# A hybrid decoder layer on one core: memory-branch gates in seven-product groups, and four of eight k-pairs by seven products in the projections and gates

## The chip, the cores and the metric

The program runs on one core of a Trainium2 chip. The core has a matrix engine (PE, TensorE), whose weight loads are listed apart as PEld, a vector engine (DVE), a scalar engine (ACT), a general engine (POOL) and a queue engine (SP) that issues the DMAs. Products accumulate in PSUM, which holds eight banks of 128 x 512 numbers; everything else on the core lies in SBUF. The metric is device time in microseconds (us), lower is better. A matmul here has a stationary operand of 128 x 128 and a moving one of 128 x 512.

## The reference

One decoder layer on 256 tokens with 2048 features. All arithmetic is float32.

```python
x = x + swiglu_half_ffn(x, ffn1_norm, ffn1_w_gate_up, ffn1_w_down)
h = rmsnorm(x, mix_norm)
u_pool, q_f, k_f, v_f, f_logit, q_m, gate_logit = jnp.split(h @ w_in, split_idx, axis=-1)
y_pool = pool_mixer(u_pool, pool_w, pool_scale) @ w_pool_up
y_fox  = forgetting_attention(rmsnorm(q_f), rmsnorm(k_f), v_f, log_f) @ w_fox_o
k_m, v_m = jnp.split(rmsnorm(mem, mem_norm) @ w_mem_kv, 2, axis=-1)
y_mem  = memory_attention(rmsnorm(q_m), rmsnorm(k_m), v_m) @ w_mem_o
g_pool, g_fox, g_mem = jnp.split(jax.nn.sigmoid(gate_logit), 3, axis=-1)
x = x + (g_pool * y_pool + g_fox * y_fox + g_mem * y_mem) @ w_out
x = x + swiglu_half_ffn(x, ffn2_norm, ffn2_w_gate_up, ffn2_w_down)
```

`w_in` is 2048 x 10768; its last 6144 columns are the three gates, 2048 columns each. The FFNs have 5632 hidden features.

## The kernel before

**Products.** The 256 tokens are two tiles of 128 (t = 0, 1). The 2048 features that a product sums over are 16 k-tiles of 128, that is eight k-pairs. A left operand is held as its high and low part (`fp32r`), and every weight tile is cut in the same way: ACT writes the high part `wh` from the loaded `raw`, DVE subtracts and writes the low part `wl` (`cut`, L238 and L239; in `mm_group` L343 and L344). One float32 product is then three matmuls, high by high, high by low and low by high. `mm_group` makes 512 columns from all k-tiles: 96 matmuls for 16 k-tiles and both token tiles, recorded at L350.

**Groups with seven products.** `pair_group` makes 2 x 512 columns at once. A k-pair, the two token tiles and the two column blocks are a 2 x 2 by 2 x 2 block product, and with sums of blocks it takes seven block products in place of eight: 21 matmuls in place of 24, all recorded at L244. The sums on the left side (`forms`) are made once for each k-pair by `form_page` (L219 to L227). The sums on the weight side are made each time: for a seven-product k-pair DVE writes `ta` (1024 columns), two halves of `tb` (512 each), and the low parts `wl` (1024), `hal` (1024), `wl` (512) and `hbl` (1024), and ACT writes the high parts `wh`, `hah`, `wh` (512) and `hbh`. A plain k-pair of the group costs DVE two `wl` of 1024. After the last seven-product k-pair ACT and four DVE operations (L314 to L318) form four terms, which L597 (projection), L905 (gates) or L387 (output) add to the four plain sums. The group holds all eight PSUM banks: four plain sums and four of the seven products.

**Which k-pairs.** The third argument from the end, an order of k-pairs, and the forms that exist set it. `MIXED = (3, 0, 4, 1, 5, 2, 6, 7)` with forms 0, 1 and 2 puts the seven-product pairs at positions 1, 3 and 5, each between plain ones. It is used for ten groups in each FFN, for the projection `kf`, for the gates of the last branch (fox) and for the second half of `w_out`.

**The order of the layer between the FFNs.** Projections `qf` (`mm_group`), `kf` (`pair_group`), `km`, the columns of the forget logits and `qm`, `vm`, `u_pool`, `vf`; then for each of three branches, in the order pool, memory, fox, and for each half of 1024 columns, the gates, their sigmoid on ACT, and `merge`: the product of the branch's output with its weight, times the gate, added to `acc`. Small work (transposes, attention, forms) waits in a queue `side`; `tick()` takes one step of it, `drain()` all. `mm_group` ticks after every two k-tiles. `pair_group` ticks twice after each plain k-pair that stands behind the last seven-product one. Behind `kf` stands a `drain()`: what is left of the transposes of the memory tokens (`memT`) and of `qf` (`qT`) is made there, and the next product, `km`, needs `memT`.

**Buffers and order.** Pages of 4 KB per partition come from a pool of 30 (x1, forms, acc, `ta`, `tb`, `hah`, `hal`, `hbh`, `hbl` and more), `raw` has 3 buffers, `wh` and `wl` 5 each, temporaries 8. Instructions are put in order on each engine by the recording layer, which runs its own model of time over them; on the chip each engine takes its list in that order.

Of the kernel before, what the change touches and what calls it, by code (L numbers as in the profile page):

```python
# [21 lines left out]
FF = 5632  # L22
NFC = FF // 512
DOWN = (2, 5, 8, 11, 14)
MIXED = (3, 0, 4, 1, 5, 2, 6, 7)
KF = FF // P
EPS = 1e-6
# [6 lines left out]
def hybrid_layer(  # L34
# [37 lines left out]
    side = deque()  # L72
# [20 lines left out]
    def temp(shape, name, dtype=F32):  # L93
        return tp.tile([P, *shape], dtype, tag="t", name=name)
# [312 lines left out]
    def form_steps(forms, tiles, n=3):  # L407
        return [lambda j=j: form_page(forms, tiles, j) for j in range(n)]
# [140 lines left out]
    cb, x1, rs, s1 = residual(s0, G_MIX, "x1")  # L549
    lx = lhs_of(x1)  # L550
# [35 lines left out]
    def project(w, c0, ncol, lhs, r, name, forms=None):  # L586
# [3 lines left out]
        else:  # L590
            buf = pages(T, [ncol], F32, name)
        if forms:
            acc, terms = pair_group(w, c0, c0 + 512, lhs, forms, MIXED)
            for g in range(2):
                for t in range(T):
                    d = terms[t, g]
                    nc.vector.tensor_tensor(d, acc[t, g], d, ALU.add)  # L597
                    nc.scalar.activation(
                        buf[t][:, g * 512 : (g + 1) * 512], d, AF.Copy, scale=r[0][:, t : t + 1]
                    )  # L600
            return buf
# [9 lines left out]
    win = w_in[0]  # L611
# [10 lines left out]
                )  # L622

    forms1 = {}
    side.extend(form_steps(forms1, x1))
    side.append(load_mem)
    side.extend(pause)
    for c in range(4):
# [238 lines left out]
    acc = pages(4, [T, 512], F32, "acc")  # L867
    mg = []
# [3 lines left out]
        (w_fox_o[0], 8, lhs_of(yf), D),  # L872
    )
    for i, (w, kt, ly, off) in enumerate(branches):
        if i == 2:
            drain()
        for c0 in range(0, 4, 2):
            gates = {}

            def sigmoid(c, src):  # L880
                gates[c] = []
                for t in range(T):
                    g = src[t] if i == 2 else temp([512], "gate")
                    nc.scalar.activation(g, src[t], AF.Sigmoid, scale=rs[0][:, t : t + 1])
                    gates[c].append(g)

# [9 lines left out]
                if i == 2:  # L896
                    side.extend(to_lhs(mg, lambda t, c=c: acc[c][:, t, :], None, "mg"))

            if i == 2:
                o = 4112 + off + c0 * 512  # L900
                pg, terms = pair_group(win, o, o + 512, lx, forms1, MIXED)
                for n in range(2):
                    for t in range(T):
                        d = terms[t, n]
# [11 lines left out]
    cb, x2, rs, s2 = residual(s1, G_FFN2, "x2")  # L916
    lg = lhs_of(mg)
    formsg, forms2 = {}, {}
    side.extend(form_steps(formsg, mg))
    for c in range(2):  # L920
        s1.load(c)
        ps = mm_group(w_out[0], c * 512, KD, lg)
        cb(c, [[ps[t][0]] for t in range(T)])
    for c in range(2, 4):
        s1.load(c)
    po, terms = pair_group(w_out[0], 1024, 1536, lg, formsg, MIXED)
    side.extend(pause * 2)
    for n in range(2):
        cb(2 + n, sums(po, terms, n))
# [41 lines left out]
```

## Time and profile before

| | |
|---|---|
| device time, three runs | 2133.16, 2136.04, 2136.01 us, median 2136.01 |
| the profiled execution | 2136.36 us, span 2134.5 us, mean granted clock 0.998 |
| PE, PEld, DVE, ACT busy | 2122.8, 1752.7, 1690.6, 1171.3 us |
| instructions on PE, DVE, ACT | 9710, 2151, 1466 |
| HBM read | 426.16 MB, 208 GB/s over the span |

The profiled execution is 1.9 us longer than its span and 0.35 us longer than the median. In a row of the timeline the first number is the start, the second the duration; in brackets stands how long the engine sat idle before it and what ended that. In the chain of work that ended last, a row is a start, a length and the line that the chain ran through. Matmuls overlap, so the time of one is read as a stretch divided by its count, not from a single row.

### The profile page before, as it was taken

What the parts mean: (1) busy time and instruction counts of PE and PEld (TensorE: products, weight loads), DVE (VectorE), ACT (ScalarE), POOL (GpSimd) and SP (SyncE); (2) the same over time, 40 slices, a digit from 0 to 9 for tenths busy, and PEclk for the clock granted to TensorE, in tenths of its full rate; (3) what the DMA queues carried; (4) which work ended last, traced back from release to release, by engine and by line L of the source; (5) the groups of instructions that cost most, each with busy time, mean ns of one, the idle gap of its engine ahead of it and who ended that gap; (6) DMA issues with size and microseconds to landing.
All of it is one profiled execution on the core that took longest, in us unless ns stands there. A gap on an engine that the chain in (4) does not pass through costs nothing.

```text
span 2134.5 us, 26003 instructions
## 1 busy us (share of the span) xinstructions
PE 2122.8 (99%) x9710; PEld 1752.7 (82%) x9710; DVE 1690.6 (79%) x2151; ACT 1171.3 (55%) x1466; POOL 3.5 (0%) x24
## 2 busy tenths in 40 slices
PE   9999999999999999999999999999999999999999
PEld 6888888888888888887788888888888888888887
DVE  6888898889858788657645778688899889989675
ACT  6555555556545565555644555555555555556453
POOL 0000000000000000000000000000000000000000
PEclk9999999999999999999999999999999999999999
DMA  7666666666866664754455656765666666677764
GB/s 257 207 207 207 207 217 208 211 230 228 272 211 205 225 203 141 255 163 158 139 195 189 195 178 212 234 224 200 210 213 205 221 208 213 206 235 246 259 190 151
DMA packets 221090, 444.66 MB, mean 208 GB/s; under 512 B 12238, under 2 KB 13348, under 8 KB 220964
## 3 DMA queue, kind: packets, MB, share of 16 engines
q1 hardware_dynamic: 220672, 442.96, 63.0%
q8 instruction: 76, 1.25, 0.2%
q14 instruction: 50, 0.41, 0.1%
q10 hardware_dynamic: 292, 0.05, 0.0%
HBM read 426.16 MB, written 16.79 MB: 208 GB/s over the span
## 4 chain that ended last, share of the span: by engine, by line
PE 99%; DVE 1%; DMA 1%; ACT 0%; issue 0%; SPq 0%; DVEq 0%; ACTq 0%
PE mm L244 68%; PE mm L350 27%; PE hid L426 1%; DMA raw<-in_ffn_w_gate_up_dram 0%; PE x L200 0%; PE fpt L849 0%; DVE wl L344 0%; PE fav L859 0%; PE mg L200 0%; PE flg L821 0%; PE mav L754 0%; PE mlg L727 0%; PE flg L819 0%; PE fav L861 0%; DVE xr L387 0%; PE fav L860 0%
## 5 line engine op out<-in xcount | busy, mean ns | idle before, releaser
L238 ACT ACTIVATE wh<-raw 128x1024 fp32r<-128x1024 f32 (+1 forms) x560 | 552.6, 989 | 580.1 <-PE mm L244 344.2
L239 DVE TENSOR_TENSOR wl<-raw,wh 128x1024 fp32r<-128x1024 f32 (+1 forms) x560 | 629.5, 1134 | 187.9 <-ACT wh L238 186.8
L244 PE MATMUL mm<-wh,x 128*128 128x512 f32 x2116 | 656.1, 391 | 0.0
L244 PEld LDWEIGHTS mm<-wh,x 128*128 128x128 f32 x2116 | 394.1, 188 | 80.0
L244 PE MATMUL mm<-wl,x 128*128 128x512 f32 x1058 | 410.9, 390 | 0.0
L344 DVE TENSOR_TENSOR wl<-raw,wh 128x1024 fp32r<-128x1024 f32 (+2 forms) x217 | 255.7, 1181 | 161.5 <-ACT wh L343 160.8
L350 PE MATMUL mm<-wh,x 128*128 128x512 f32 (+1 forms) x1216 | 371.9, 384 | 3.0 <-ACT wh L343 1.7
L244 PE MATMUL mm<-wh,hid 128*128 128x512 f32 x1168 | 357.8, 390 | 0.0
L343 ACT ACTIVATE wh<-raw 128x1024 fp32r<-128x1024 f32 (+2 forms) x217 | 221.1, 1024 | 237.4 <-PE mm L350 183.2
L350 PEld LDWEIGHTS mm<-wh,x 128*128 128x128 f32 x1216 | 224.7, 188 | 48.4 <-issue 2.9
L244 PEld LDWEIGHTS mm<-wh,hid 128*128 128x128 f32 x1168 | 218.8, 188 | 45.2
L244 PEld LDWEIGHTS mm<-wl,x 128*128 128x128 f32 x1058 | 198.6, 188 | 41.9
L350 PE MATMUL mm<-wl,x 128*128 128x512 f32 (+1 forms) x608 | 231.5, 382 | 0.5 <-DVE wl L344 0.5
L244 PE MATMUL mm<-wl,hid 128*128 128x512 f32 x584 | 222.4, 389 | 0.0
L350 PEld LDWEIGHTS mm<-wl,x 128*128 128x128 f32 x608 | 114.5, 188 | 21.6 <-DVE wl L344 1.0
L290 DVE TENSOR_TENSOR ta<-raw 128x1024 f32<-128x1024 f32 x92 | 112.3, 1220 | 20.5 <-DMA raw<-in_ffn_w_gate_up_dram 8.0
L244 PEld LDWEIGHTS mm<-wl,hid 128*128 128x128 f32 x584 | 109.6, 188 | 22.7
L238 ACT ACTIVATE hah<-ta 128x1024 fp32r<-128x1024 f32 x92 | 96.9, 1053 | 37.5 <-DVE ta L290 37.5
L239 DVE TENSOR_TENSOR hal<-ta,hah 128x1024 fp32r<-128x1024 f32 x92 | 112.4, 1222 | 3.4 <-ACT hah L238 3.4
L239 DVE TENSOR_TENSOR hbl<-tb,hbh 128x1024 fp32r<-128x1024 f32 x92 | 112.3, 1221 | 0.1
L244 PE MATMUL mm<-hah,form 128*128 128x512 f32 x368 | 111.3, 389 | 0.0
L238 ACT ACTIVATE hbh<-tb 128x1024 fp32r<-128x1024 f32 x92 | 96.8, 1052 | 21.9 <-DVE tb L296 21.9
(324 smaller groups left out, 2143.3 us busy)
## 6 DMA issues: line engine op xcount, KB each, us to landing
raw<-in_ffn_w_gate_up_dram SPq DMA_DIRECT2D x321, 512.0 KB, 4.0
raw<-in_ffn_w_down_dram SPq DMA_DIRECT2D x176, 512.0 KB, 5.5
raw<-in_w_in_dram SPq DMA_DIRECT2D x52, 1024.0 KB, 5.0
raw<-in_w_in_dram SPq DMA_DIRECT2D x48, 512.0 KB, 4.2
raw<-in_ffn_w_gate_up_dram SPq DMA_DIRECT2D x15, 1024.0 KB, 7.3
hd<-hf SPq DMA_DIRECT2D x20, 512.0 KB, 5.2
hg<-hd SPq DMA_DIRECT2D x20, 512.0 KB, 8.4
raw<-in_w_mem_kv_dram SPq DMA_DIRECT2D x8, 1024.0 KB, 7.6
```

The lines of the kernel that those rows point to most:

```text
L238: nc.scalar.activation(dst[0], src, AF.Copy)
L239: nc.vector.tensor_tensor(dst[1], src, dst[0].bitcast(F32), ALU.subtract)
L244: nc.tensor.matmul(ps, sides[part], wt[i][:, col : col + 512], start=start and q == 0, stop=stop and q == 2)
L290: nc.vector.tensor_tensor(ta, s[:, 3:4, :].to_broadcast([P, 2, 512]), s[:, 1:3, :], ALU.add)
L343: nc.scalar.activation(hv, rv, AF.Copy)
L344: nc.vector.tensor_tensor(lv, rv, hv.bitcast(F32), ALU.subtract)
L350: nc.tensor.matmul(ps[t][i][:, :n], lhs(k, part, t), wt[:, kk, o : o + n], start=k == 0 and q == 0, stop=k == kt - 1 and q == 2,)
L426: nc.tensor.transpose(ps[:, j, t * P : (t + 1) * P], hd[t][:, k * P : (k + 1) * P], ident)
```

## The change

The memory branch (i = 1) takes its gates through `pair_group`, as the fox branch does, with the sigmoid written over the terms. A new order `HALF = (4, 0, 5, 1, 6, 2, 3, 7)` with a fourth form puts seven-product pairs at positions 1, 3, 5 and 6; the `kf` projection, the gates of the memory and fox branches and the second half of `w_out` use it. The FFNs keep `MIXED` and three forms. The drain that stood before the third branch stands before the second and the third.

```diff
+HALF = (4, 0, 5, 1, 6, 2, 3, 7)
...
         if forms:
-            acc, terms = pair_group(w, c0, c0 + 512, lhs, forms, MIXED)
+            acc, terms = pair_group(w, c0, c0 + 512, lhs, forms, HALF)
...
-    side.extend(form_steps(forms1, x1))
+    side.extend(form_steps(forms1, x1, 4))
...
-        if i == 2:
+        if i > 0:
             drain()
...
-                    g = src[t] if i == 2 else temp([512], "gate")
+                    g = src[t] if i > 0 else temp([512], "gate")
...
-            if i == 2:
+            if i > 0:
                 o = 4112 + off + c0 * 512
-                pg, terms = pair_group(win, o, o + 512, lx, forms1, MIXED)
+                pg, terms = pair_group(win, o, o + 512, lx, forms1, HALF)
...
-    side.extend(form_steps(formsg, mg))
+    side.extend(form_steps(formsg, mg, 4))
...
-    po, terms = pair_group(w_out[0], 1024, 1536, lg, formsg, MIXED)
+    po, terms = pair_group(w_out[0], 1024, 1536, lg, formsg, HALF)
```

One line is added at the top, so a line of the changed kernel is one higher than the same line before. In the built programs PE has 9604 matmuls and transposes before and 9568 after, DVE 2153 and 2241 instructions, ACT 1408 and 1436, SP 753 and 769. The 16 more on SP are loads of the memory gates, cut in 512 KB pieces instead of 1 MB.

Three places show how the order moves. First DVE at the end of `kf`: `raw_6624` holds the third seven-product pair, `ta_6631`, `tb_6632`, `hal_6635` and `hbl_6645` are made from it, `wl_6887` to `wl_6943` are the weights of `km`, and the row of L315 is the first term. Before:

```order
L570 TENSOR_TENSOR qf_5984<-qf_5984,qfy_6402 128x1024
L239 TENSOR_TENSOR hal_6635<-ta_6631,hah_6634 128x1024
L295 TENSOR_TENSOR tb_6632<-ta_6631,raw_6624 128x512
L239 TENSOR_TENSOR wl_6757<-raw_6727,wh_6756 128x1024
L344 TENSOR_TENSOR wl_6887<-raw_6884,wh_6886 128x1024
L296 TENSOR_TENSOR tb_6632<-tb_6632,raw_6624 128x512
L344 TENSOR_TENSOR wl_6903<-raw_6884,wh_6902 128x1024
L239 TENSOR_TENSOR hbl_6645<-tb_6632,hbh_6644 128x1024
L190 SCALAR_TENSOR_TENSOR memT_6717<-memT_6718,cols_108,memT_6717 128x256 x2
L344 TENSOR_TENSOR wl_6921<-raw_6918,wh_6920 128x1024
L315 TENSOR_TENSOR u3_6670<-mm_6502,ua_6669 128x512
```

After, from the same `hbl_6645` on; `raw_6669` holds the fourth seven-product pair, `raw_6904` and `raw_6938` hold weights of `km`:

```order
L240 TENSOR_TENSOR hbl_6645<-tb_6632,hbh_6644 128x1024
L291 TENSOR_TENSOR ta_6676<-raw_6669 128x1024
L345 TENSOR_TENSOR wl_6907<-raw_6904,wh_6906 128x1024
L345 TENSOR_TENSOR wl_6923<-raw_6904,wh_6922 128x1024
L240 TENSOR_TENSOR hal_6680<-ta_6676,hah_6679 128x1024
L296 TENSOR_TENSOR tb_6677<-ta_6676,raw_6669 128x512
L345 TENSOR_TENSOR wl_6941<-raw_6938,wh_6940 128x1024
L345 TENSOR_TENSOR wl_6963<-raw_6938,wh_6962 128x1024
L297 TENSOR_TENSOR tb_6677<-tb_6677,raw_6669 128x512
L240 TENSOR_TENSOR hbl_6690<-tb_6677,hbh_6689 128x1024
L191 SCALAR_TENSOR_TENSOR memT_6742<-memT_6743,cols_108,memT_6742 128x256 x2
L316 TENSOR_TENSOR u3_6715<-mm_6502,ua_6714 128x512
```

A whole further set of sums now stands between `hbl` of the third pair and the first term, with four weight cuts of `km` in between.

Second PE at the same place: the last matmuls of `kf` (`hbl,form` closes a product that the terms need), then the transposes `memT` and `qT`, then `km`. Before:

```order
L244 MATMUL mm<-hbl,form 128x512
L244 MATMUL mm<-hbl,x_5319 128x512
L244 MATMUL mm<-wh,x_6093 128x512 x2
L244 MATMUL mm<-wl,x_6093 128x512
L244 MATMUL mm<-wh,x_6093 128x512 x2
L244 MATMUL mm<-wl,x_6093 128x512
L244 MATMUL mm<-wh,x_6119 128x512 x2
L244 MATMUL mm<-wl,x_6119 128x512
L244 MATMUL mm<-wh,x_6119 128x512 x2
L244 MATMUL mm<-wl,x_6119 128x512
L200 MATMUL memT<-ident,mraw 128x128 x12
L580 MATMUL qT<-ident,qf 128x128 x16
```

After:

```order
L245 MATMUL mm<-hah,form 128x512 x4
L245 MATMUL mm<-hal,form 128x512 x2
L245 MATMUL mm<-hbh,form 128x512 x2
L245 MATMUL mm<-hbh,x_5345 128x512 x2
L245 MATMUL mm<-hbl,form 128x512
L245 MATMUL mm<-hbl,x_5345 128x512
L245 MATMUL mm<-wh,x_6119 128x512 x2
L245 MATMUL mm<-wl,x_6119 128x512
L245 MATMUL mm<-wh,x_6119 128x512 x2
L245 MATMUL mm<-wl,x_6119 128x512
L201 MATMUL memT<-ident,mraw 128x128 x16
L581 MATMUL qT<-ident,qf 128x128 x16
```

The fourth pair's sums are used 12 matmuls before the end of the group, six matmuls stand behind the last of them instead of twelve, and 16 transposes of `memT` instead of 12 stand before `qT`.

Third DVE in the memory gates. Before, where one merge ends and the next gates begin:

```order
L344 TENSOR_TENSOR wl_9920<-raw_9917,wh_9919 128x1024
L344 TENSOR_TENSOR wl_9936<-raw_9917,wh_9935 128x1024
L894 TENSOR_TENSOR gate_9837<-mm_9841,gate_9837 128x512
L894 TENSOR_TENSOR gate_9839<-mm_9842,gate_9839 128x512
L895 TENSOR_TENSOR acc_8189<-acc_8189,gate_9837 128x512
L895 TENSOR_TENSOR acc_8189<-acc_8189,gate_9839 128x512
L344 TENSOR_TENSOR wl_9954<-raw_9951,wh_9953 128x1024
L344 TENSOR_TENSOR wl_9970<-raw_9951,wh_9969 128x1024
L344 TENSOR_TENSOR wl_9988<-raw_9985,wh_9987 128x1024
L344 TENSOR_TENSOR wl_10004<-raw_9985,wh_10003 128x1024
```

After, in the middle of the first memory group, where the third and fourth seven-product pairs (`raw_9558`, `raw_9603`) follow each other:

```order
L291 TENSOR_TENSOR ta_9565<-raw_9558 128x1024
L240 TENSOR_TENSOR wl_9543<-raw_9523,wh_9542 128x1024
L240 TENSOR_TENSOR wl_9562<-raw_9558,wh_9561 128x1024
L240 TENSOR_TENSOR wl_9573<-raw_9558,wh_9572 128x512
L240 TENSOR_TENSOR hal_9569<-ta_9565,hah_9568 128x1024
L296 TENSOR_TENSOR tb_9566<-ta_9565,raw_9558 128x512
L240 TENSOR_TENSOR wl_9607<-raw_9603,wh_9606 128x1024
L297 TENSOR_TENSOR tb_9566<-tb_9566,raw_9558 128x512
L240 TENSOR_TENSOR wl_9618<-raw_9603,wh_9617 128x512
L240 TENSOR_TENSOR hbl_9579<-tb_9566,hbh_9578 128x1024
```

DVE's list there turns from weight cuts alone into cuts mixed with sums, and the cuts of the fourth pair stand among the sums of the third.

## Rows read from the trace of the kernel before

**Rows 1.** The page's part 1: busy us, share of the span, instructions.

```profile
PE 2122.8 (99%) x9710; PEld 1752.7 (82%) x9710; DVE 1690.6 (79%) x2151; ACT 1171.3 (55%) x1466; POOL 3.5 (0%) x24
```

**Rows 2.** The page's part 4: the chain that ended last, by engine.

```profile
PE 99%; DVE 1%; DMA 1%; ACT 0%; issue 0%; SPq 0%; DVEq 0%; ACTq 0%
```

**Rows 3.** Chain of the gates and merges: start, length, line, matmuls.

```profile
1062.01 147.37 PE mm L350 x649
1209.38 41.48 PE mm L244 x183
```

**Rows 4.** Stretches: us, then busy us by engine, granted clock, DMA share, GB/s.

```profile
1100.00:1209.00 109.00, 109.00 (x483) 90.28 (x482) 61.78 (x61) 48.96 (x50) 0.00 (x0) 1.00 0.60 193
1508.81:1551.26 42.45, 42.45 (x193) 35.15 (x192) 37.40 (x42) 24.11 (x28) 0.00 (x0) 1.00 0.66 211
766.87:808.72 41.85, 41.85 (x188) 34.54 (x188) 39.05 (x54) 24.89 (x31) 0.00 (x0) 1.00 0.60 200
816.00:818.00 2.00, 2.00 (x6) 1.55 (x5) 2.00 (x5) 2.00 (x5) 0.00 (x0) 0.50 0.00 0
```

**Rows 5.** Chain around the end of kf.

```profile
766.87 32.93 PE mm L244 x145
...
813.38 0.70 DVE u L597
...
814.13 0.66 PE qT L580 x4
814.79 3.60 PE mm L350 x8
```

**Rows 6.** Timeline of PE at the end of kf.

```profile
808.72 1.47 PE L200 MATMUL memT<-ident,mraw 128*128 128x128 f32 x12
810.68 1.26 PE L580 MATMUL qT<-ident,qf 128*128 128x128 f32 x8 [0.50 <-DVE u L317]
813.40 1.38 PE L580 MATMUL qT<-ident,qf 128*128 128x128 f32 x8 [1.47 <-DVE uv L318]
814.73 0.68 PE L350 MATMUL mm<-wh,memT 128*128 128x512 f32 x1
```

**Rows 7.** Timeline of DVE in kf, from the first seven-product pair's ta.

```profile
767.31 1.22 DVE L290 TENSOR_TENSOR ta<-raw 128x1024 f32<-128x1024 f32 x1
...
795.84 1.22 DVE L239 TENSOR_TENSOR hal<-ta,hah 128x1024 fp32r<-128x1024 f32 x1
796.98 0.69 DVE L295 TENSOR_TENSOR tb<-ta,raw 128x512 f32<-128x512 f32 x1
797.58 1.22 DVE L239 TENSOR_TENSOR wl<-raw,wh 128x1024 fp32r<-128x1024 f32 x1
...
801.83 1.22 DVE L239 TENSOR_TENSOR hbl<-tb,hbh 128x1024 fp32r<-128x1024 f32 x1
...
806.89 0.68 DVE L315 TENSOR_TENSOR u<-mm,ua 128x512 f32<-128x512 f32 x1
...
813.99 0.68 DVE L597 TENSOR_TENSOR uv<-mm,uv 128x512 f32<-128x512 f32 x1
```

**Rows 8.** Timeline of ACT in kf.

```profile
797.38 1.06 ACT L343 ACTIVATE wh<-raw 128x1024 fp32r<-128x1024 f32 x1 [3.10 <-DMA raw<-in_w_mem_kv_dram]
...
800.57 1.06 ACT L238 ACTIVATE hbh<-tb 128x1024 fp32r<-128x1024 f32 x1
```

**Rows 9.** Timeline of SP: loads of the memory weights.

```profile
792.24 10.06 SPq L331 DMA_DIRECT2D raw<-in_w_mem_kv_dram  x4
```

**Rows 10.** The page's part 6: issues, KB each, median us to landing.

```profile
raw<-in_w_mem_kv_dram SPq DMA_DIRECT2D x8, 1024.0 KB, 7.6
```

**Rows 11.** Timeline of DVE at the end of w_out.

```profile
1413.96 0.69 DVE L315 TENSOR_TENSOR u<-mm,ua 128x512 f32<-128x512 f32 x1 [0.51 <-PE mm L244]
...
1430.06 0.68 DVE L387 TENSOR_TENSOR xr<-uv,xr 128x512 f32<-128x512 f32 x1
```

**Rows 12.** Timeline of PE at the end of w_out.

```profile
1437.67 1.47 PE L200 MATMUL x<-ident,xr 128*128 128x128 f32 x12
```

## The prediction, written before the changed kernel was run

> **What bounds the kernel now.** The page's busy times come first: PE works 99% of the span, its weight loads 82%, DVE 79%, and the span has 9710 PE instructions [rows 1]. The chain that ended last says the same: 99% of it runs through PE [rows 2]. So a matmul taken away is worth its own time, wherever PE is not then made to wait for somebody else. The price is a stretch of the chain divided by its count: 147.37 us over 649 matmuls of `mm_group` is 0.2271 us, 41.48 us over 183 of `pair_group` is 0.2267 us [rows 3]. The question is whether PE stays fed, and by whom. The stretches show who is next behind PE [rows 4]. In a pass of plain gates (1100 to 1209) DVE is busy 61.78 of 109 us, 57%. In a group of FFN2 with three seven-product pairs it is busy 37.40 of 42.45 us, 88%, and in `kf` 39.05 of 41.85 us, 93%; in all three PE is busy every microsecond. So seven-product pairs spend DVE's reserve, and at 93% it still just holds.
>
> The one place that the change touches where PE does wait today is the end of `kf`. The chain leaves PE there for DVE's last adds [rows 5]. PE's timeline shows how: the last matmul of `kf` ends at about 808.7, twelve `memT` transposes follow, then eight `qT` transposes wait 0.50 us for `u` of L317 and eight more wait 1.47 us for `uv` of L318 [rows 6]. All eight PSUM banks are held by four sums and four products; a bank comes free only when DVE has read it into a term or an add. `km` starts at 814.73, right behind DVE's last add, which runs from 813.99 for 0.68 us [rows 7].
>
> **The change part by part.** *Matmuls.* PE loses 36: three in `kf`, 24 in the memory gates (two passes of 192 become 180), six in the fox gates, three in `w_out`. By 0.2267 us they are worth 8.16 us. I take the three of `kf` out, since DVE sets that group's end (below): 33 x 0.2267 = 7.5 us of gain.
>
> The Trainium skill (TensorE: Matmul & The Clock Gate, section Back-to-back issue gap) gives about 131 ns as the sustained spacing of matmuls of 512 columns in a real kernel. By that figure 33 matmuls would be worth an estimated 4.3 us. The trace does not agree: 649 of them in one gapless row took 227 ns each [rows 3], and the measurement decides.
>
> *Memory and fox gates.* One DVE operation of 1024 columns costs 1.14 us (795.84 to 796.98), one of 512 columns 0.60 us (796.98 to 797.58) [rows 7]. A seven-product pair takes four of the first and three of the second, 6.4 us; a plain pair takes two, 2.3 us. On PE a seven-product pair is 21 x 0.2267 = 4.8 us, a plain one 5.4 us. A memory pass (180 matmuls of gates, 48 of the merge) is then 228 x 0.2267 = 51.7 us of PE. DVE's list over it has 28 operations of each size: 28 x 1.14 + 28 x 0.60 = 48.7 us, 94%. This is what `kf` carries now with PE gapless [rows 4]. The doubtful point is the third and fourth pair side by side (third place of the order): walking both lists with these prices, every DVE product still stands some 3 to 6 us ahead of the matmul that uses it, the least at `hbl` of the fourth pair. I take 0; what hides it is the 57% of the pass before, in which PE is fed so easily that the buffers are full when the gates begin. Without that cover it costs what rival two says. A fox pass has 62.6 us of PE and, by the same count, at most 54.3 us of DVE, 87%, so 0 there. The 16 more loads on SP are the same bytes in halves: 0.
>
> *The drains.* The one that now stands before the memory branch finds an empty list, since the fox attention's steps are all taken in the pool branch: 0. The extra form step costs DVE and ACT a few short operations in stretches of 57% load: 0.
>
> *The end of `kf`.* Here DVE has no reserve. From the first `ta` at 767.31 to the end of the third pair's `hbl`, which starts at 801.83 [rows 7], 35.7 us passed. The list holds 23 operations of 1024 and 8 of 512 columns there, 31.0 us, which leaves 4.7 us for 16 short operations and the waits. In the changed order the list up to the *fourth* pair's `hbl` holds 27 and 11: 37.4 us. With the same 4.7 us it ends at 767 + 42.1 = 809. Two more waits are likely. ACT's `hbh` takes 1.06 us [rows 8] and stands between `tb` and `hbl`, with nothing else left in DVE's list: 1.1 us. And `wl_6907`, a weight cut of `km`, stands ahead of the fourth pair's sums (first place of the order). Its load can start only when the last plain pair has left its buffer, at about 795.5. Today's first `km` load was issued at 792.24 [rows 9], and ACT, which waited 3.10 us for it, began its `wh` at 797.38 [rows 8]: 5.1 us. So the load lands at 800.6, `wh` is done at 801.7, and DVE stands there at 800.9 or so: 1.0 us. `hbl` then ends at 811.0, while PE, which without any wait would end `kf` at 808.4, stands idle behind it for five to six microseconds.
>
> From there: today 7.84 us pass from the first term at 806.89 [rows 7] to `km`, that is eight operations of 0.60, two weight cuts of 1.14, one `memT` and 0.35 us between them. Afterwards it is eight of 0.60, one weight cut, the first eviction of `qT` (16 `memT` transposes before it instead of 12 use up a bank more, so `km` has to wait for that) and the 0.35: 7.0 us. Ahead of it stand two `memT` scalings of 256 columns, 0.8 us (I take 0.4 each, below the 0.60 of 512 columns). `km` starts at 811.0 + 0.8 + 7.0 = 818.8 instead of 814.73: **+4.1 us**. The ends: if no wait of DVE outlasts PE, PE's own end of 808.4 sets the terms and `km` starts at about 814.3, -0.4; if the load takes the 7.6 us that is the median of these loads [rows 10], everything stands 2.5 us later, +6.6. I stay in the middle, since 5.1 us is the row of this very load. PE that has idled so long comes back slowly: after today's waits the stretch 816 to 818 has a granted clock of 0.50 [rows 4], 1.2 of 2.4 GHz, and eight matmuls of `km` took 3.60 us, 0.45 each [rows 5]. The closing matmul of the last product is among the first after the idle time: +0.4. `km` itself begins at that clock today too: 0.
>
> *`w_out`.* Its first term is at 1413.96, its last sum at 1430.06 + 0.68 [rows 11], 16.8 us; the transposes that need the sums stand on PE at 1437.67 [rows 12], 23.7 us behind the first term. One plain pair less behind the last product takes 24 x 0.2267 = 5.4 us of that cover and leaves 18.3. Cost 0 with 1.5 us to spare; the upper end, if the fourth pair holds up the terms by 3 us, is 1.5 us.
>
> *Sum.* -7.5 (33 matmuls) + 4.1 + 0.4 (end of `kf`) + 0 (gates, `w_out`) = -3.0 us. The profiled execution goes from 2136.36 to 2133.4 us. It stands 0.35 us over the median of 2136.01, so the forecast is 2133.0 us.
>
> **The rivals.** *One: the end of `kf` swallows the fourth pair.* The waits inside today's 35.7 us are partly waits of a DVE that ran ahead and was stopped; with more in its list they would vanish. `km` then starts between 814.3 and 816, and the sum lies between -7.9 and -4.3: 2128.1 to 2131.7. For it speaks that PE is gapless at 93% today [rows 4]; against it that DVE's plain sum alone, 37.4 us and some 2 us of short operations, ends at 806.5, with 2 us left for every wait.
>
> *Two, slower: the memory passes become DVE's.* Each has 48.7 us of DVE work against 51.7 us on PE. If the four `hbh` waits of 1.06 us lie bare and DVE waits otherwise at about the rate of `kf`'s list (some 2.4 of the 4.7 us, over 33 us of work, makes 3.5 us), a pass takes 48.7 + 4.2 + 3.5 = 56.4 us, 4.7 more than PE needs. It decides from 3.0 us of waits in a pass on. Two passes make +9.3, with the rest -3.0 + 9.3 = +6.3: 2142.3 us. Against it stand the 88% and 93% passes without a gap [rows 4] and the distance in the order. The Trainium skill (Perfetto Trace Analysis, section Identifying the Most-Contended Engine) holds that matmul busy time misjudges how near PE is to its limit and wants the weight loads' share read in its place. By that share PE stands at 82% against DVE's 79%, nearly level, which speaks for this rival; the trace gives both numbers [rows 1], and no run yet shows what more DVE work does.
>
> *Three: the gain is eaten.* The load of `km` comes late (+6.6) and `w_out` stalls (+1.5): -7.5 + 6.6 + 0.4 + 1.5 = +1.0, 2137.0 us.
>
> That the change does nothing is ruled out by the order: the matmuls are gone.
>
> **How the numbers follow.** Forecast (`km` 2 to 5 us later): 0.52. Rival one: 0.33. Rival two: 0.08. Rival three: 0.07. About 0.2%, 4.3 us, is what a measurement here tells from no change: faster means below 2131.7, slower above 2140.3. Faster is rival one and the very edge of the forecast, 0.35; slower is rival two, 0.08; the rest, 0.57, is the same. The range, 2128.5 to 2137.5, takes in the forecast, nearly all of rival one and rival three; rival two and the edges, under 0.2, stay out.
>
> **What would show it.** Right: `km` starts 3 to 5 us later against the start of `kf`, PE idles behind `hbl` of the fourth pair, its clock is 0.50 there, and the memory passes are gapless on PE with 51 to 52 us each and DVE over 90%. Rival one: no idle time within `kf`, and the terms follow PE. Rival two: idle time of PE before `hal` or `hbl` matmuls in the memory passes, released by DVE. Rival three: a long DMA wait of ACT before a weight cut of `km`, and idle time before the transposes of `x` behind `w_out`. The forecast is wrong altogether if a matmul's price falls with the mixture, or if a place that I put at 0 shows idle time of PE above 2 us.

## The result: slower, and not where the prediction looked

The changed kernel takes 2146.53 us (median of 6 runs, 2145.31 to 2147.77), against 2136.03 for the kernel before: a ratio of 1.0053, interval 1.0043 to 1.0063: half a per cent slower. The forecast was 2133.0, the range ended at 2137.5, and even the slower rival stopped at 2142.3. The profiled execution has a span of 2145.8 us, 11.3 more than before.

The page of the changed kernel, parts 1 and 4, stands against [rows 1, 2]:

```profile
PE 2121.6 (99%) x9674; PEld 1748.0 (81%) x9674; DVE 1749.5 (82%) x2239; ACT 1188.8 (55%) x1494; POOL 3.5 (0%) x24
PE 95%; DVE 2%; DMA 2%; ACT 1%; issue 1%; SPq 0%; ACTq 0%; DVEq 0%
```

PE's share looks unchanged, but the chain has left PE for 5% of the span, where it was 1%. Loads and DVE cuts now stand in the chain. PE's waits by cause (us in all, how often, the longest):

```profile
PE mm L245 <- ACT hbh L239: 10.3, 3, 3.8
...
PE mm L245 <- DVE hal L240: 0.9, 2, 0.4
PE mm L245 <- ACT hah L239: 0.9, 2, 0.5
```

In the kernel before no matmul of L244 waited for `hah`, `hal` or `hbh`. Three places hold these waits. PE's timeline of the changed kernel, at the end of `kf`, in the second memory pass and in the second fox pass (in brackets the idle time before and what ended it):

```profile
804.18 1.19 PE L245 MATMUL mm<-hah,form 128*128 128x512 f32 x4 [0.46 <-ACT hah L239]
805.81 0.73 PE L245 MATMUL mm<-hal,form 128*128 128x512 f32 x2 [0.44 <-DVE hal L240]
810.37 1.22 PE L245 MATMUL mm<-hbh,form 128*128 128x512 f32 x2 [3.83 <-ACT hbh L239]
...
1200.83 1.22 PE L245 MATMUL mm<-hbh,form 128*128 128x512 f32 x2 [2.69 <-ACT hbh L239]
...
1315.55 1.19 PE L245 MATMUL mm<-hah,form 128*128 128x512 f32 x4 [0.39 <-ACT hah L239]
1317.18 0.73 PE L245 MATMUL mm<-hal,form 128*128 128x512 f32 x2 [0.44 <-DVE hal L240]
1321.75 1.22 PE L245 MATMUL mm<-hbh,form 128*128 128x512 f32 x2 [3.83 <-ACT hbh L239]
```

It is the fourth seven-product pair each time. To see what each stage gained or lost, the same events were read off PE's timeline in every kernel, those of the experiments below included: the first matmul of `kf` and of `km`, the end of the last matmul of the pool branch and of each memory and fox pass, the first matmul on a form in `w_out` and in FFN2. The table gives how much later (+) each comes than in the kernel before. The difference of two columns is what a stage cost. The columns by themselves say less: three of the executions came to FFN1's first matmul on a form 1.3 to 1.5 us earlier than the kernel before, and keep that lead.

| kernel | `kf` | `km` | pool ends | memory 1 | memory 2 | fox 1 | fox 2 | `w_out` pair | FFN2 | span |
|---|---|---|---|---|---|---|---|---|---|---|
| changed | -0.4 | +5.1 | +3.4 | +0.7 | +4.0 | +3.7 | +11.6 | +11.6 | +11.0 | +11.3 |
| memory gates in threes | -0.3 | -0.3 | -0.3 | -2.4 | -4.4 | -4.4 | -4.4 | -4.4 | -4.4 | -4.3 |
| four pairs, memory plain | -0.2 | +5.3 | +3.7 | +3.7 | +3.7 | +3.0 | +2.0 | +2.5 | +1.8 | +1.8 |
| pairs apart | -2.0 | +6.4 | +4.8 | +3.6 | +6.3 | +5.8 | +11.3 | +11.4 | +10.7 | +10.7 |
| cuts behind | -1.8 | +4.3 | +2.6 | -0.1 | -1.8 | +1.7 | +0.7 | +1.1 | +0.5 | +0.5 |
| four raw buffers | -0.1 | +4.8 | +3.1 | +2.0 | -0.1 | -1.3 | 0.0 | 0.0 | -0.5 | -0.1 |
| four cut buffers | +2.7 | +9.9 | +8.3 | +6.0 | +6.5 | +8.2 | +9.9 | +9.8 | +9.4 | +11.2 |
| `kf` in threes | -0.4 | -0.4 | -0.5 | -3.2 | +1.3 | +0.5 | +8.1 | +8.2 | +7.5 | +7.8 |
| memory threes, fox fours | -1.3 | -1.1 | -1.8 | -3.9 | -5.9 | -6.6 | -7.5 | -7.0 | -7.6 | -7.6 |

In the changed kernel the first memory pass gains 2.7 us, all that its twelve matmuls are worth. The second loses 3.3 where it should gain 2.7; the second fox pass loses 7.9 where it should gain 0.7. Those two places cost 14.5 us against plan.

### The profile page after: what moved, and what is told of

The parts are those of the page before. It is cut to its first block, busy times and chain, and to the rows that moved or that the text cites. A ratio compares the mean times of both kernels' runs of the same rounds, so it can differ in the third digit from the quotient of the medians.

```text
span 2145.8 us, 26086 instructions
## 1 busy us (share of the span) xinstructions
PE 2121.6 (99%) x9674; PEld 1748.0 (81%) x9674; DVE 1749.5 (82%) x2239; ACT 1188.8 (55%) x1494; POOL 3.5 (0%) x24
## 4 chain that ended last, share of the span: by engine, by line
PE 95%; DVE 2%; DMA 2%; ACT 1%; issue 1%; SPq 0%; ACTq 0%; DVEq 0%
PE mm L245 69%; PE mm L351 22%; PE hid L427 1%; DVE wl L345 1%; DMA raw<-in_ffn_w_gate_up_dram 0%; DVE wl L240 0%; PE x L201 0%; DMA raw<-in_w_in_dram 0%; DMA raw<-in_w_mem_o_dram 0%; PE fpt L850 0%; DMA raw<-in_w_mem_kv_dram 0%; DMA raw<-in_w_fox_o_dram 0%; ACT wh L344 0%; PE fav L860 0%; ACT hbh L239 0%
## 5 line engine op out<-in xcount | busy, mean ns | idle before, releaser
L239 ACT ACTIVATE wh<-raw 128x1024 fp32r<-128x1024 f32 x592 | 580.5, 984 | 600.4 <-PE mm L245 346.0
L240 DVE TENSOR_TENSOR wl<-raw,wh 128x1024 fp32r<-128x1024 f32 x592 | 659.9, 1126 | 186.5 <-ACT wh L239 185.9
L245 PE MATMUL mm<-wh,x 128*128 128x512 f32 x2240 | 694.6, 392 | 0.0
L245 PEld LDWEIGHTS mm<-wh,x 128*128 128x128 f32 x2240 | 418.7, 188 | 85.4
L245 PE MATMUL mm<-wl,x 128*128 128x512 f32 x1120 | 433.8, 390 | 0.0
L345 DVE TENSOR_TENSOR wl<-raw,wh 128x1024 fp32r<-128x1024 f32 (+2 forms) x185 | 215.1, 1171 | 98.9 <-ACT wh L344 98.0
L351 PE MATMUL mm<-wh,x 128*128 128x512 f32 (+1 forms) x960 | 292.1, 383 | 3.2 <-ACT wh L344 1.8
L344 ACT ACTIVATE wh<-raw 128x1024 fp32r<-128x1024 f32 (+2 forms) x185 | 185.8, 1017 | 170.4 <-PE mm L351 117.7
L351 PEld LDWEIGHTS mm<-wh,x 128*128 128x128 f32 x960 | 176.6, 189 | 38.4 <-issue 2.9
L351 PE MATMUL mm<-wl,x 128*128 128x512 f32 (+1 forms) x480 | 181.6, 380 | 0.5 <-DVE wl L345 0.5
L240 DVE TENSOR_TENSOR hbl<-tb,hbh 128x1024 fp32r<-128x1024 f32 x104 | 126.8, 1220 | 11.4 <-ACT hbh L239 11.4
```

Of the source, the lines that this page charges most:

```text
L239: nc.scalar.activation(dst[0], src, AF.Copy)
L240: nc.vector.tensor_tensor(dst[1], src, dst[0].bitcast(F32), ALU.subtract)
L245: nc.tensor.matmul(ps, sides[part], wt[i][:, col : col + 512], start=start and q == 0, stop=stop and q == 2)
L344: nc.scalar.activation(hv, rv, AF.Copy)
L345: nc.vector.tensor_tensor(lv, rv, hv.bitcast(F32), ALU.subtract)
L351: nc.tensor.matmul(ps[t][i][:, :n], lhs(k, part, t), wt[:, kk, o : o + n], start=k == 0 and q == 0, stop=k == kt - 1 and q == 2,)
```

## How the wait arises

The chain of the changed kernel through the second memory pass (start, length, line):

```profile
1175.96 7.85 DMA raw<-in_w_in_dram
...
1183.92 1.07 ACT wh L239
...
1185.01 1.24 DVE wl L240
...
1186.27 5.27 DMA raw<-in_w_mem_o_dram
...
1191.62 1.07 ACT wh L344
...
1193.86 0.82 DVE wl L345
...
1196.81 2.27 DVE wl L345 x2
1199.08 0.61 DVE tb L297
1199.71 1.07 ACT hbh L239
1200.83 1.22 PE mm L245 x2
```

And DVE's timeline at the same place, from `ta` of the fourth pair on:

```profile
1189.11 1.22 DVE L291 TENSOR_TENSOR ta<-raw 128x1024 f32<-128x1024 f32 x1
1192.71 2.36 DVE L345 TENSOR_TENSOR wl<-raw,wh 128x1024 fp32r<-128x1024 f32 x2 [2.38 <-ACT wh L344]
1194.99 1.22 DVE L240 TENSOR_TENSOR hal<-ta,hah 128x1024 fp32r<-128x1024 f32 x1
1196.13 0.68 DVE L296 TENSOR_TENSOR tb<-ta,raw 128x512 f32<-128x512 f32 x1
1196.73 2.35 DVE L345 TENSOR_TENSOR wl<-raw,wh 128x1024 fp32r<-128x1024 f32 x2
1199.00 0.68 DVE L297 TENSOR_TENSOR tb<-tb,raw 128x512 f32<-128x512 f32 x1
1200.80 1.23 DVE L240 TENSOR_TENSOR hbl<-tb,hbh 128x1024 fp32r<-128x1024 f32 x1 [1.12 <-ACT hbh L239]
```

PE's timeline shows what it waits for meanwhile (`ym` is the left operand of the merge):

```profile
1192.73 0.49 PE L351 MATMUL mm<-wh,ym 128*128 128x512 f32 x1 [0.32 <-ACT wh L344]
1193.99 0.50 PE L351 MATMUL mm<-wl,ym 128*128 128x512 f32 x1 [0.76 <-DVE wl L345]
```

Read together: `ta` is done at 1190.3. The next things in the lists of ACT and DVE are not `hah` and `hal`, which have what they need, but two cuts of the *next* product, the merge's weight `w_mem_o`. Their load was issued at 1186.27, right behind a weight cut of this group that ended at 1186.25, and took 5.27 us; a second load, for the merge after it, followed at 1186.87, right behind the third pair's second `tb`. (The expectations below speak of the third pair's buffer alone; for the first load the trace shows the cut.) So DVE stands idle for 2.38 us, makes two cuts of the merge (2.28 us), then `hal`, then half of `tb`, then two cuts of the second merge (2.27 us), and at last `hbl`. Some 7 us pass between `ta` and `hbl` that the fourth pair does not need. In this pass PE's own list has a part of the merge ahead of the fourth pair, so PE waited for the first two cuts as well (0.32 and 0.76 us). The same pattern stands at the end of `kf` and in the second fox pass: DVE 1.24 and 2.28 us idle in front of those two cuts. The first fox pass has it too (1.47 us idle) but loses only 0.4 us: there PE's list has merge matmuls ahead of the fourth pair's `hbh`, from 1249.9 to 1257.3, which cover the wait. In the second memory pass these last from 1192.7 to 1197.7, which is too short, and in the second fox pass there are none; there and in `kf` the cuts that stand in front are not needed until the next product begins, 5 us and more behind the fourth pair's `hbh`.

PE pays twice: it waits, and it comes back at half speed. Stretches of the changed kernel (columns as in [rows 4]): the whole second memory pass, then the stretches behind the three waits.

```profile
1155.70:1213.36 57.66, 53.89 (x229) 43.69 (x229) 49.38 (x57) 29.71 (x33) 0.00 (x0) 0.97 0.56 182
1200.00:1204.00 4.00, 3.17 (x8) 2.58 (x9) 1.86 (x2) 0.77 (x1) 0.00 (x0) 0.57 0.88 283
1321.70:1327.50 5.80, 5.75 (x17) 4.60 (x18) 5.01 (x8) 1.65 (x3) 0.00 (x0) 0.57 0.94 355
810.40:814.00 3.60, 3.60 (x9) 2.83 (x10) 3.02 (x5) 0.76 (x2) 0.00 (x0) 0.50 1.01 389
```

In the memory pass PE is idle 3.8 us, and the granted clock of 0.57 in the second stretch (between the levels of 1.2 and 2.4 GHz) costs 3.17 x 0.43 = 1.4 us. In the second fox pass it is 4.7 us idle and 5.75 x 0.43 = 2.5 us of clock. That is 5.2 of the 6.0 and 7.2 of the 8.5 us that the two passes lose against plan.

What a trace can't tell is which of three things has to go: the place of the cuts in the lists (**Q**, queue), the late load behind three buffers (**B**), or simply the amount of DVE work (**C**, capacity, the prediction's rival two; the first four expectations call it L, load).

## Experiments

**Each half of the change alone.** First the memory gates in groups, with three pairs in the old order:

```diff
-                pg, terms = pair_group(win, o, o + 512, lx, forms1, HALF)
+                pg, terms = pair_group(win, o, o + 512, lx, forms1, MIXED)
...
-            acc, terms = pair_group(w, c0, c0 + 512, lhs, forms, HALF)
+            acc, terms = pair_group(w, c0, c0 + 512, lhs, forms, MIXED)
```

(the same in `w_out`, and three forms everywhere).

> Only the first half of the change: the memory gates go through seven-product groups, with the old order and three forms, as kf, the fox gates and w_out keep them. Theory Q (queue): PE waits in the changed kernel because, on ACT and DVE, the first two cuts of the next product stand between ta and hal of the fourth seven-product pair, and their load is issued only when the third pair, directly ahead, gives up its raw buffer. With three pairs that row does not occur (the last hal stands directly behind its ta), so PE should not wait in the gates, 18 matmuls less are worth 18 x 0.2267 = 4.1 us, and the time is 2132 us (2130.5 to 2133.5). Theory L (load): DVE has too much work in the memory passes as such, and PE waits for the sum of it. A memory pass then has 24 + 21 operations (some 40 us) on 52 us of PE and would still fit: 2132 us by L too; a time above 2136 would speak against both.

Measured: 2131.25 us, ratio 0.9979 (0.9970 to 0.9988). Its 18 matmuls came out whole: 4.1 us. Then four pairs without the memory groups (the condition changes in the same way at the drain and at the sigmoid):

```diff
-            if i > 0:
+            if i == 2:
                 o = 4112 + off + c0 * 512
```

> Only the second half of the change: four seven-product pairs in the new order in kf, the fox gates and w_out, while the memory gates stay plain. In the order of this kernel the next product's cuts stand behind hal of the fourth pair in both fox passes, but between ta and hal in kf. Q: kf costs what it does in the changed kernel (3.4 us behind vf, its three matmuls included), the fox passes run without waits (6 matmuls, -1.4 us) and w_out gains 0.65 us: +1.4, 2137.4 us (2136 to 2139). L: the fox passes carry the same DVE work as in the changed kernel and lose the same 8.6 us there, against -1.4 for their matmuls: about 2145 us.

Measured: 2136.96 us, ratio 1.0010 (1.0001 to 1.0018). By the table `kf` costs the same as in the changed kernel, and both fox passes *gain*, 0.7 and 1.1 us. The second does so with the DVE work that goes with a loss of 8.5 us against plan in the changed kernel:

```profile
1276.57:1340.60 64.03, 64.03 (x288) 52.90 (x288) 59.09 (x79) 35.30 (x38) 0.00 (x0) 1.00 0.59 197
```

DVE is busy 59.09 of 64.03 us, 92%, and PE never waits. C as the sum of work in a pass is hit: the same pass, but in an order where the next product's cuts stand behind `hal`. The first load of that product also went out earlier, 24 us behind the start of the pass (1300.35) where it was 30 us in the changed kernel (1307.29), so this run does not tell Q from B. Neither half holds the large loss alone; it needs both.

**The third and fourth pair apart.**

```diff
-HALF = (4, 0, 5, 1, 6, 2, 3, 7)
+HALF = (4, 0, 1, 5, 2, 6, 3, 7)
```

> The changed kernel with the seven-product pairs at positions 1, 2, 4 and 6 instead of 1, 3, 5 and 6: the same work on every engine, the same single plain pair at the end, but a plain pair between the third and the fourth. The raw buffer that the next product's first load takes is now that of a plain pair, which is given up sooner. Q: the load is issued earlier, the wait on it goes or shrinks, and most of the loss in the second memory pass and the second fox pass (5.5 and 7.5 us) goes with it: 2134 to 2141 us, with kf's end still late by some 3 us. L: DVE's work in every pass is the same, so the time stays at 2146 us within 1.5.

Measured: 2147.40 us, ratio 1.0060 (1.0048 to 1.0073). Q missed, as it was stated, but the edit did not do what it was for. In the second memory pass the first load of the next product was issued at 1190.41, right behind the third pair's second `tb`, that is 31.8 us behind the end of the pass before; in the changed kernel it was 30.6. In `kf` it came 2.8 us later, counted from the first matmul of `kf`, and only in the second fox pass 0.8 us earlier. So this run is no test of an earlier load. DVE in the second memory pass of this kernel:

```profile
1192.66 1.22 DVE L291 TENSOR_TENSOR ta<-raw 128x1024 f32<-128x1024 f32 x1
1195.01 1.23 DVE L240 TENSOR_TENSOR hal<-ta,hah 128x1024 fp32r<-128x1024 f32 x1 [1.13 <-ACT hah L239]
1196.15 0.69 DVE L296 TENSOR_TENSOR tb<-ta,raw 128x512 f32<-128x512 f32 x1
1196.75 2.36 DVE L345 TENSOR_TENSOR wl<-raw,wh 128x1024 fp32r<-128x1024 f32 x2
1199.02 0.69 DVE L297 TENSOR_TENSOR tb<-tb,raw 128x512 f32<-128x512 f32 x1
1200.30 2.36 DVE L345 TENSOR_TENSOR wl<-raw,wh 128x1024 fp32r<-128x1024 f32 x2 [0.59 <-ACT wh L344]
1202.58 1.22 DVE L240 TENSOR_TENSOR hbl<-tb,hbh 128x1024 fp32r<-128x1024 f32 x1
```

Here the first load is no longer waited for before `hal`, because the cuts have moved behind it; a bare wait for `hah` has come in, and the second load is waited for (0.59 us). In `kf` and in the second fox pass the two cuts still stand ahead of `hal`, with waits of 2.22 and 1.11 us. So setting the pairs apart is no cure. What is common to both kernels is four cuts of the next products ahead of the last low part, 4.7 us of them.

**All sums of the fourth pair first.** The fourth pair's operations and the next product's first cuts are pinned behind what was written before them on their engine:

```diff
+            keep = tc.keep_in_program_order if order is HALF and last else (lambda q: q)
...
-            cut(hb, tb.rearrange("p s c -> p (s c)"))
+            cut(hb, tb.rearrange("p s c -> p (s c)"), keep)
...
+                keep = tc.keep_in_program_order if behind and k0 + h0 < 8 else (lambda q: q)
```

> The changed kernel with one thing moved: in kf and all gates and w_out, ACT and DVE make all sums and cuts of the fourth seven-product pair (ta, hah, hal, tb, hbh, hbl) ahead of the next product's first cuts. No instruction is added or taken away. Q: PE's waits before hah, hal and hbh of the fourth pair go in the second memory pass and the fox passes, and nearly so in kf, where hbl ends some 5 us earlier; the 36 matmuls come out as time, less up to 2 us at kf and where the next product's first cuts are now late: 2127.9 to 2131 us. L: DVE does the same work in each pass, PE waits as long, in other places: 2144 to 2148 us.

Measured: 2173.37 us, ratio 1.0179 (1.0165 to 1.0193), far outside both. The waits before `hah` and `hal` did go, and of those before `hbh` only 0.9 us in `kf` is left. But the pin went further than meant: it put the next product's cuts behind the sigmoids of the gates too. ACT and PE at the end of the first memory pass:

```profile
1155.49 0.70 ACT L887 ACTIVATE uv<-uv,x1y 128x512 f32<-128x512 f32 x1
1156.10 3.88 ACT L346 ACTIVATE wh<-raw 128x1024 fp32r<-128x1024 f32 x4
...
1157.20 1.22 PE L353 MATMUL mm<-wh,ym 128*128 128x512 f32 x2 [5.42 <-ACT wh L346]
```

The loads had been issued from 1135.19 on, twenty microseconds ahead; the cuts stood in line, and PE waited 5.4 to 6.0 us in each of the four passes and 8.0 us at `km`. It is the same kind of fault with the roles changed, and it shows what places in the lists can cost by themselves: no instruction more, 27 us more than the changed kernel. As a test of Q against C it is inconclusive.

**The cuts directly behind the fourth pair.** So the order was set by one link: the next product's first four cuts (in a memory pass two, since a merge there has no more) behind `hbh` (ACT) and `hbl` (DVE) of the fourth pair, and behind nothing else.

```diff
-            cut(hb, tb.rearrange("p s c -> p (s c)"))
+            ahead[:] = cut(hb, tb.rearrange("p s c -> p (s c)"))
...
+                if behind and k0 + h0 < 8:
+                    for i, prev in zip(own, ahead):
+                        tc.add_manual_dep(i.ins, prev.ins.name, link, reason="behind")
```

> The changed kernel with one thing moved: behind kf and the memory and fox gates the next product's first four cuts may be issued on ACT and DVE only behind hbh and hbl of the fourth seven-product pair; they then stand directly behind it, among the terms, and not behind the sigmoids as in the run before, where each next product began 5.4 us late. Same instructions. Q (the place of the cuts is the cause): the waits of PE before hah, hal and hbh go, and no new wait of over 2 us comes: 2128 to 2132 us. C (capacity: DVE's list in a memory or fox pass, with the waits for ACT that belong to it, is longer than PE's, in whatever order): PE's idle time comes back at the head of the next product or in the first pairs of the next gates, 2143 to 2149 us.

Measured: 2137.83 us, ratio 1.0013 (1.0004 to 1.0022). This lies in neither range, 5.8 us above Q's and 5.2 below C's, so the place of the time has to decide. It is 8.7 us less than the changed kernel, whose excess was 10.5, with no instruction added or removed. From the end of the pool branch to FFN2 the changed kernel loses 7.6 us, this one gains 2.1: the second memory pass now gains 1.7 us, the second fox pass 1.1. In the second memory pass the merge's first load went out 29.7 us behind the end of the pass before (1184.55), 0.9 us earlier than in the changed kernel, and of PE's wait before `hbh` 0.59 of 2.69 us are left. So there the place of the cuts does it, with a load that is nearly as late. What stays is `kf`, with 6.1 us lost from its first matmul to `km` where the changed kernel loses 5.5, and a first fox pass that loses 3.5. In `kf` new waits have taken the old one's place:

```profile
804.68 0.73 PE L250 MATMUL mm<-hbh,form 128*128 128x512 f32 x2 [1.06 <-ACT hbh L243]
...
811.15 0.66 PE L201 MATMUL memT<-ident,mraw 128*128 128x128 f32 x4 [2.65 <-DVE ua L608]
814.41 1.97 PE L201 MATMUL memT<-ident,mraw 128*128 128x128 f32 x8 [2.60 <-DVE u L323]
```

Counted from the first matmul of `kf`, `hbh` comes 4.2 us earlier than in the changed kernel, but now the cuts stand among the terms, and the transposes wait for terms and sums that free their PSUM banks late. In neither order does DVE's work at the end of `kf` fit. In the first fox pass DVE works without a pause from 1205 to 1229 and PE waits 1.75 us for the last `hbh`; there C seems to have a share, which no run here separates.

**A fourth raw buffer,** and its counterpart. The space comes from `wh` and `wl`, so a second kernel has only that part:

```diff
-            raw = wp.tile([P, 2, 2, 512], F32, tag="raw", name="raw")
+            raw = wp.tile([P, 2, 2, 512], F32, tag="raw", name="raw", bufs=4)
...
-            wp.tile([P, n], F32R, tag="wh", name="wh", bufs=5),
+            wp.tile([P, n], F32R, tag="wh", name="wh", bufs=4),
```

> The changed kernel with four raw buffers instead of three, and four wh and four wl instead of five each, since the space has to come from there. B (buffers: the next product's first load is late because the third pair still holds its buffer): the loads go out a block earlier, no cut of the next product waits for its load any more, and kf, the second memory pass and the second fox pass lose at most a third of what they did: 2129 to 2136 us, and well below the next run. C: 2143 to 2149 us, since DVE's work is the same.

> The counterpart of the run before: three raw buffers as in the changed kernel, and four wh and four wl instead of five. It tells what the smaller number of cut buffers does by itself. B: it stalls as the changed kernel does, 2144 to 2152 us. C: the same, 2144 to 2152 us. If it comes out near 2130, the cut buffers and the order that they lead to are the cause, and not the raw buffers.

Measured: with four raw buffers 2135.55 us, ratio 1.0003 (0.9994 to 1.0012); the counterpart 2147.59 us, ratio 1.0058 (1.0045 to 1.0071). The two are 12.0 us apart, and B's range is hit both times, but the table shows that the counterpart came to its time in another way. It is 2.7 us late before `kf` begins, since fewer cut buffers cost time outside the gates too, and `kf` loses 7.1 us. From the end of the pool branch to FFN2 it loses 1.1 us, where the changed kernel loses 7.6. That the two totals agree is chance. DVE in its second fox pass, where `hal` now stands ahead of the next product's cuts:

```profile
1315.74 1.23 DVE L240 TENSOR_TENSOR hal<-ta,hah 128x1024 fp32r<-128x1024 f32 x1 [1.13 <-ACT hah L239]
1317.65 2.36 DVE L345 TENSOR_TENSOR wl<-raw,wh 128x1024 fp32r<-128x1024 f32 x2
```

DVE in the second memory pass with four raw buffers:

```profile
1190.17 1.22 DVE L291 TENSOR_TENSOR ta<-raw 128x1024 f32<-128x1024 f32 x1
1191.30 1.22 DVE L345 TENSOR_TENSOR wl<-raw,wh 128x1024 fp32r<-128x1024 f32 x1
1192.52 1.23 DVE L240 TENSOR_TENSOR hal<-ta,hah 128x1024 fp32r<-128x1024 f32 x1
```

The weights are there, and DVE no longer idles before a cut of the next product. The order has changed with the buffers, too: two of the cuts now stand ahead of the fourth pair's `hah`, one behind `hal`. `kf` still loses 4.9 us, against B. From the end of the pool branch to FFN2 this kernel gains 3.6 us, 4.7 more than its counterpart; the rest of the 12 us lies in `kf` and in the stages outside the gates, which use the same buffers. So from the pool branch's end to FFN2 a fourth buffer takes 11.2 us off the changed kernel, and fewer cut buffers alone, with the order that they lead to, take 6.5 of them. How much of the loss is the wait for the load and how much the place of the cuts stays open: a kernel with the changed one's order and an earlier load was not tried, since the order follows from when loads can start.

**More DVE work, without the pattern.** To the kernel with threes in the memory gates four DVE operations per pass are added:

```diff
                     cut(wt, raw[:, n, :, :].rearrange("p k c -> p (k c)"))
+                    if u in again:
+                        nc.vector.tensor_tensor(
+                            wt[1], raw[:, n, :, :].rearrange("p k c -> p (k c)"), wt[0].bitcast(F32), ALU.subtract
+                        )
```

> The kernel with only the memory gates in groups of three seven-product pairs (2131.25 us), plus four more DVE operations of 1024 columns in each memory pass, beside the seven-product pairs: the low cut of two plain pairs is made twice, with the same values. DVE's list in a pass goes from 26 x 1.14 + 25 x 0.60 = 44.6 to 49.2 us against 52.4 us on PE, 94%, the share that the fourth pair gives it in the changed kernel (48.7 of 51.7). Q: no cut of a next product stands in front of a late sum, so nothing is lost: 2130 to 2133 us. C: a pass at 94% is over what DVE can do with its waits, and the second memory pass at least loses some 5 us: 2135 to 2142 us.

Measured: 2130.69 us, ratio 0.9981 (0.9971 to 0.9990), the same as without them (2131.25). Its second memory pass:

```profile
1150.85:1203.22 52.37, 52.37 (x233) 43.38 (x232) 48.68 (x56) 28.61 (x31) 0.00 (x0) 1.00 0.61 199
```

DVE is busy 48.68 of 52.37 us, 93%, and PE has no gap. In the changed kernel's pass, 57.66 us long, DVE was busy 49.38. The work is nearly the same; only there PE waits. C as a limit on the share falls. The added operations wait for no load and add no work to ACT, so this run does not speak of DVE's waits for ACT.

**`kf` put back,** with everything else as changed:

```diff
-            acc, terms = pair_group(w, c0, c0 + 512, lhs, forms, HALF)
+            acc, terms = pair_group(w, c0, c0 + 512, lhs, forms, MIXED, (0, 1, 2))
...
+    side.append(lambda: form_page(forms1, x1, 3))
     side.append(lambda: pool_window(0))
```

> The changed kernel with kf put back to the old order and three seven-product pairs; memory gates, fox gates and w_out keep four. The fourth form page is made behind kf. Q: what kf lost goes (3.8 us with the half clock behind it: km starts where it did before), and the second memory pass and the second fox pass lose as in the changed kernel, since the order still has two cuts of the next product between ta and hal there: 2142 to 2144 us. If the late end of kf were what makes the later passes late (a chain of lateness from kf on), the time would fall to 2128 to 2132 us.

Measured: 2143.43 us, ratio 1.0038 (1.0025 to 1.0052). Lateness is not handed on from `kf`: the second memory pass loses 4.5 us and the second fox pass 7.6, much as in the changed kernel (3.3 and 7.9).

**What can be kept.** `kf` as before, threes in the memory gates, fours in the fox gates and `w_out`:

```diff
+                pg, terms = pair_group(win, o, o + 512, lx, forms1, *((MIXED, (0, 1, 2)) if i == 1 else (HALF,)))
```

> What the runs so far let one keep: kf as before, the memory gates in groups of three (old order), the fox gates and the second half of w_out in groups of four (new order). In the order of this kernel no cut of a next product stands ahead of hal of the last seven-product pair. Q: 18 + 6 + 3 = 27 matmuls come out as time, 27 x 0.2267 = 6.1 us: 2128 to 2130.5 us. C (DVE too full where memory groups are followed by fox groups of four): the fox passes lose some 3 us or more: 2131 to 2136 us.

Measured: 2128.59 us, ratio 0.9968 (0.9956 to 0.9981), faster than the kernel before by 6.7 us: 27 matmuls by 0.2267 are 6.1. Its first fox pass with what follows, then its second fox pass, four seven-product pairs behind memory groups:

```profile
1204.00:1267.00 63.00, 63.00 (x283) 52.25 (x282) 53.47 (x61) 34.04 (x38) 0.00 (x0) 1.00 0.62 200
1266.95:1331.20 64.25, 64.25 (x288) 52.94 (x288) 59.10 (x79) 35.30 (x38) 0.00 (x0) 1.00 0.59 197
```

PE is without a gap, at full clock, with DVE at 85 and 92%.

## The prediction, step by step

- **Matmuls: right.** The price of 0.2267 us held wherever PE did not wait: 4.1 us for 18 matmuls, 2.7 for the twelve of the first memory pass, 0.65 for the three of `w_out`. The figure of 131 ns from the Trainium skill (TensorE: Matmul & The Clock Gate, section Back-to-back issue gap) would have made the 18 worth 2.4 us; the measurement speaks against it here.
- **End of `kf`: right in mechanism and nearly in size.** `hbl` of the fourth pair was put at 811.0 and ended at 811.6; `km` was put at 818.8 and started at 819.8. The wait for the load of `km` was seen and was the row that bound: the load was put behind the last cut of a plain pair at about 795.5, and was issued at 795.90, right behind such a cut. Not seen: `km` itself then ran without the half clock of before. There the chain had 3.60 us for the first eight matmuls [rows 5]; afterwards it has 22.06 us for 96 at once. So 1.6 us came back by the end of the pool branch, which is 3.4 us late where 4.5 were forecast.
- **`w_out`: right.** No cost, 0.65 us gained.
- **Memory and fox gates at 0: the step that failed.** "Walking both lists with these prices, every DVE product still stands some 3 to 6 us ahead" counted DVE's operations, but not the load that an operation in the list waits for. In `kf` the prediction had put exactly that together: a cut of the next product ahead of the fourth pair's sums, its load issued only when a buffer comes free, 5.1 us to land. The same rows of the order stood in the second memory pass and in both fox passes, with other names, and were not walked in that way. What the runs showed in place of the 0: two cuts of the next product ahead of `hal`, a wait for their load of 2.38 and 2.28 us, two more cuts ahead of `hbl`, and PE idle for 3.8 and 4.7 us, with the half clock behind it. The lead was real at first: in the second memory pass the first pair's `hbl` was ready 8.5 us before PE began with that pair's `hbh`, the second 2.8, the third 1.7; the fourth ended 1.2 us behind PE's start. So the lead had fallen below the 3 us of the walk before the first cut of the next product came; this part is not explained by that cut. Two passes at a loss of 6.0 and 8.5 us are the miss.
- **Rival two had the sign, but not the cause.** It made DVE's sum of work and waits exceed PE's, at 4.7 us in *each memory* pass. The first memory pass lost nothing, the second fox pass lost most, and the same work cost nothing in other orders. The count of at most 54.3 us of DVE for a fox pass, 87%, was short: in two kernels where PE did not wait the second one holds 59.1 us, 92%. The Trainium skill (Perfetto Trace Analysis, section Identifying the Most-Contended Engine) would judge how much room PE has left by the share of peak at which it computes and by the share of its weight loads. By the latter PE and DVE were nearly level, 82 and 79%; DVE at 93% beside a gapless PE shows that a share of busy time did not decide here.
- **The range** left out the case altogether, since the only slower case was priced as an overflow of work in the memory passes, without a load in the list and without the half clock behind each wait.

## What to carry to other kernels

When an edit makes a weight block stay longer in its buffer, ask which load now starts later, and then which instructions in the in-order lists stand *behind* the first use of that load: they are late too, though all their own inputs are there. Walk each list with the landing time of every load, at every place where the pattern occurs, not only where the engine is known to be short. A DVE share of 93% was free here, and a pass with 49.38 of 57.66 us, 86%, lost six.

## Not expected of the hardware

A wait of PE of 3.8 us cost another half to two thirds of that: behind it the granted clock was 0.50 over 3.60 us in `kf` and 0.57 over 5.80 us in the second fox pass, an estimated 1.8 and 2.5 us. And between kernels with the same instructions on every engine, only their order changed, the time went from 2137.8 to 2146.5 to 2173.4 us.
